# Two-layer decoder trunk: the gated y of both query halves split in the next head's first pass, and TensorE in place of transfers for turning the attention weights of the last two and a half heads

## The chip, the cores and the metric

The kernel runs on one core of one Trainium2 chip. The metric is the device time of one execution in microseconds (us), as the median of several runs. A core has a matrix engine (TensorE, PE in the profile, with its weight loads as PEld), VectorE (DVE), ScalarE (ACT), GpSimd (POOL), a queue engine that issues transfers (SyncE, SP), and 16 DMA engines that carry them. Each engine works through its own queue in order and waits on semaphores for the others.

## What is computed

Two pre-norm residual layers on x (1024 rows of 1024 float32), then a final RMSNorm. The change lies wholly in the second layer, gated attention with a forgetting bias:

```python
def fox_mixer(h, w_in, b_f, w_out):              # 16 heads of width 64
    u = h @ w_in                                 # q, k, v, gate, f_logit
    cum = jnp.cumsum(jax.nn.log_sigmoid(f_logit + b_f), axis=1)
    logits = einsum("bqhd,bkhd->bhqk", q, k) * scale
    logits = logits + (cum[q] - cum[k])          # causal mask after it
    p = jax.nn.softmax(logits, axis=-1)
    o = einsum("bhqk,bkhd->bqhd", p, v)
    y = o * jax.nn.silu(gate)
    return y @ w_out
```

The first layer is a gated linear recurrence (RG-LRU) with three large projections. It takes the time up to about 440 us and isn't touched.

## The kernel before

**Arithmetic.** Products of float32 are made of fp32r parts: a value is split into a high part, a cast (`to_hi`, line 87 on ACT), and a low part, a subtraction of the cast from the value (`to_lo`, line 98). A product is three matmuls: high by high, high by low, low by high (`gps`, `ups`, `vps`, `ops`). The attention weights are split into `ph` and `pl` and multiplied by V in one precision, so they need two.

**Heads, halves and passes.** Attention goes over 16 heads (`hd`); two heads make a pair and share 128 partitions. Each head has two query halves, `c` = 0 and 1, of 512 rows in four blocks of 128. For one half, `maxima` (line 750) makes the logits `S` from `T` (keys) and `U` (queries) on TensorE, adds the mask and takes row maxima on DVE (line 773), and takes the exponential on ACT (line 778), which also gives the row sums. Row tiles are `p` for the two shorter rows of a half and `pp` for the two longer ones. `weigh` (line 815) then turns the weights so that keys lie on partitions, splits them (lines 87 and 98) and multiplies them by V into `O`. The loop over heads runs two passes per head: in the first, `weigh(hd, 0)` stands beside `maxima(hd, 1)`; in the second, `weigh(hd, 1)` beside `maxima(hd+1, 0)`.

**How weights are turned.** Two ways exist. TensorE transposes 128x128 blocks into `pt` (helper on line 61). Or `turn_row` (line 726): DVE transposes 32x32 blocks (`STREAM_TRANSPOSE`, line 733), SP writes the tile to device memory (`turnd`, line 738 for c = 1 and 740 for c = 0), and four reads bring it back into `pp` with the blocks in place (line 745). `by_dma` (line 721) says which halves use the second way for their two longer rows; before, it was all but head 0's first half. The two shorter rows always go by TensorE.

**Gate and y.** At the end of a head the row sums are inverted, transposed (line 791), copied to `rc`, written to memory (`recd`, line 794) and read back as a broadcast over partitions (`recb`, line 803). POOL then multiplies the gate `sg` by it (`scale`, line 813), and, after the odd head of a pair, `yo` by the gate (`gated`, line 911). `yo` is the half's output: ACT copies one head's part of `O` into it (line 901), DVE adds the other. There are two buffers of the tag `yo`, one for each half; the next pair's even head writes into them again.

**Putting y away.** For the pairs of heads up to 11, `put_away` (line 917) splits y: ACT casts `yh` from `yo`, DVE subtracts in place in `yo`, and SP writes both parts to `y1d` (line 928). In head 12 `load_y` (line 984) brings them back as `yhh` and `yhl`. The pairs of heads 13 and 15 are split in place (`split_y`, line 979). `partial` (line 998) multiplies y of the first six pairs by the output weights (`wo1`, loads `wf<-in_wo`), adds the residual (`xp`, read on line 1006, added on 1009, stored on 1010). `turned` (line 1029) transposes the result, adds the last two pairs and takes the squares for the norm.

**What sets the order.** The generators `weigh` and `maxima` are stepped by strings (`ORDER` for heads up to 11, `LAST` from 12 on): "0" and "1" step one of the two, and "." steps the projections that fill TensorE in between, and then a `side` generator.

```python
ORDER = "1.0.1.10.1..0", "10.1.0.10.1.0.0"
LAST = "1..0.1..10..1..0", "10..1.0..10..1.0..0"
```

Before, the side generator of a second pass is `settle` (line 930): it fetches the sums at its third ".", scales and gates the first half at its fourth, and puts that half away at its fifth. The side generator of a first pass is `put_later` (line 941): at its fourth "." it puts away the second half of the head before. Both matter only behind odd heads up to 11. All transfers of this layer go out of SP's one queue, in the order of the program, over eight DMA semaphores in rotation. Tiles of the tags `wf` (three buffers), `S` and `R` (two) are shared by many steps.

Of the kernel before, what the change touches and what calls it, by code (L numbers as in the profile page):

```python
# [17 lines left out]
P = 128  # L18
SEQ = 1024
HALF = 512  # L20
# [13 lines left out]
def f32(ap):  # L34
    return ap.bitcast(F32)
# [3 lines left out]
def trunk(ctx: ExitStack, tc: tile.TileContext, xt, w0, wg, wo0, pc, gn, gf, w1, wv, wf, bf, wo1, out):  # L39
# [44 lines left out]
    def to_hi(hi, src, eng, scale=None):  # L84
        if eng is nc.scalar:
            if scale is None:
                nc.scalar.copy(hi, src)  # L87
            else:
                nc.scalar.activation(hi, src, AF.Copy, scale=scale)
        elif eng is nc.gpsimd:  # L90
            nc.gpsimd.tensor_scalar(hi, src, 1.0 if scale is None else scale, 0.0, ALU.mult, ALU.add)
        elif scale is None:
            eng.tensor_copy(hi, src)
        else:
            eng.tensor_scalar(hi, src, scale, None, ALU.mult)

    def to_lo(lo, src, hi, eng):
        return eng.tensor_tensor(lo, src, f32(hi), ALU.subtract)  # L98
# [80 lines left out]
    with ExitStack() as l0:  # L179
# [33 lines left out]
        first = ([], [])  # L213
# [288 lines left out]
    with ExitStack() as l1:  # L502
# [170 lines left out]
        first = values(0, [])  # L673
# [45 lines left out]
            return two_rows[c][:, r * size : r * size + n]  # L719

        def by_dma(hd, c):
            return hd > 0 or c == 1

        written, turns = [None], {}

# [73 lines left out]
        def fetch_sums(hd, b0=0, b1=8):  # L799
            pair, s = hd // 2, hd % 2  # L800
            if s == 0:
                recs[pair] = at.tile([P, SEQ], F32, tag="recb", name="recb", bufs=1)
            nc.sync.dma_start(
                recs[pair][s * HD : (s + 1) * HD, b0 * P : b1 * P],
                recd[hd : hd + 1, b0:b1].rearrange("o b q -> o (b q)").to_broadcast([HD, (b1 - b0) * P]),
            )

        def scale(hd, cs=slice(0, SEQ)):
            rows = slice((hd % 2) * HD, (hd % 2 + 1) * HD)
            for b in range(cs.start, cs.stop, HALF):  # L810
                part = slice(b, b + HALF)
                sg = sgs[hd // 2][rows, part]
                nc.gpsimd.tensor_tensor(sg, sg, recs[hd // 2][rows, part], ALU.mult)  # L813

        def weigh(hd, c, sub=slice(0, HALF)):
# [6 lines left out]
            O = ps.tile([P, HALF], F32, tag="O", name="O")[:, : sub.stop - sub.start]  # L822
            b = 4 * c

            def cover(r):
                first = [max(j, r) for j in range(r + 2)]
                return [(j, (q - b) * P, (r + 2 - q) * P) for j, q in enumerate(first)]

            def packed(pieces):
                units = []  # L830
                for piece in pieces:
                    if not units or sum(w for _, _, w in units[-1]) + piece[2] > HALF:
                        units.append([])
                    units[-1].append(piece)
                return units

            mine = cover(b) if sub.start == 0 else []
            away = cover(b + 2) if sub.stop == HALF else []
            n = len(away) - 1 if by_dma(hd, c) else 0
            mine, away = packed(mine + away[n:]), packed(away[:n])  # L840
            steps = [(z[i : i + 2], z is away) for z in (mine, away) for i in range(0, len(z), 2)]
            count = [0, 2 * sum(map(len, mine + away))]

# [21 lines left out]
            for units, far in steps:  # L865
# [4 lines left out]
                for u, unit in enumerate(units):  # L870
                    n = sum(w for _, _, w in unit)
# [28 lines left out]
            r0, r1 = s * HD, (1 - s) * HD  # L900
# [4 lines left out]
        def gated(hd, c, sub=slice(0, HALF)):  # L905

            if hd % 2 == 0:
                return
            pair = hd // 2
            yo = yos[pair, c][:, sub]  # L910
            nc.gpsimd.tensor_tensor(
                yo, yo, sgs[pair][:, c * HALF + sub.start : c * HALF + sub.stop], ALU.mult
            )
            if hd == 15:
                split_y(c, pair, yo, sub)

        def put_away(hd, c):
            if hd % 2 == 0 or hd > 12:
                return
            pair = hd // 2  # L920
            yo = yos[pair, c]
            yh = at.tile([P, HALF], F32R, tag="xp", name="yh", bufs=2)
            with tc.issue_after(seen[0].ins):
                to_hi(yh, yo, nc.scalar)
            with tc.issue_after(masked[0].ins):
                to_lo(yo.bitcast(F32R), yo, yh, nc.vector)
            for part, y in enumerate((f32(yh), yo)):
                nc.sync.dma_start(y1d[c, pair, part], y)

        def settle(hd):  # L930
            yield
            yield
            with tc.issue_after(written[0].ins):
                fetch_sums(hd)
            yield
            scale(hd)
            gated(hd, 0)
            yield
            put_away(hd, 0)

        def put_later(hd):
            yield
            yield
            yield
            put_away(hd, 1)

        def beside(*gens):
            for _ in itertools.zip_longest(*gens):
# [167 lines left out]
        for hd in range(HEADS):  # L1116
# [20 lines left out]
            first, second = LAST if hd > 11 else ORDER  # L1137
            side = put_later(hd - 1) if hd else iter(())
            run(first, weigh(hd, 0), maxima(hd, 1), fill=fill, side=side)
            drain(side)  # L1140
            if hd == HEADS - 1:
# [106 lines left out]
```

## Time and profile before

| | before |
|---|---|
| runs (us) | 1132.59, 1134.2, 1134.7 |
| median (us) | 1134.2 |
| profiled execution's own time (us) | 1137.31 |
| span in the profile (us) | 1135.5 |
| mean granted TensorE clock | 0.981 |
| busy, share of the span | PE 97%, PEld 82%, DVE 70%, ACT 51%, POOL 15% |
| device memory read / written | 87.02 / 39.65 MB |

The profile is of one execution. Times in its rows are us from the start of the span. "Busy" counts an engine's instructions from start to end; the time of an instruction that waits is idle time of its engine, and the releaser named beside it is what ended the wait. A matmul row names its output and its two operands, with the size of the weights and of the moving tile. The chain of waits is the work that ended last, followed back from the end. The granted clock is TensorE's, as a share of full speed.

### The profile page before, as it was taken

The numbers are of one execution on the slowest core, as the hardware profiler recorded it, in microseconds if no ns is written. First come the engines' busy times: TensorE is split into PE (matmuls) and PEld (weight loads), VectorE is DVE, ScalarE is ACT, GpSimd is POOL, SyncE is SP. The second block draws the span as 40 slices with busy tenths as digits, with TensorE's granted clock in tenths as the row PEclk, the third lists the DMA queues.
The fourth block names the chain that finished last, engine by engine and source line by source line (L and its number), as shares of the span: only waits on it lengthen the run. The fifth ranks groups of instructions, "written<-read, shape, count | busy, mean of one in ns | idle before, by whom it ended". The sixth has DMA issues, their size and how long they took to land.

```text
span 1135.5 us, 15920 instructions
## 1 busy us (share of the span) xinstructions
PE 1097.4 (97%) x5627; PEld 928.5 (82%) x5627; DVE 797.6 (70%) x1291; ACT 581.6 (51%) x1038; POOL 171.8 (15%) x120
## 2 busy tenths in 40 slices
PE   9999999999999999999999999899998999988998
PEld 7787888888888888978788988788887898867776
DVE  8898765677566897667787487874777847647545
ACT  8587344445445656445555355554555534424335
POOL 2312212212111102311111011101111010110010
PEclk9999999999999999999999999999998999989899
DMA  5111111111112124355767267672676735897554
GB/s 217 59 61 41 53 42 52 47 51 53 41 52 66 45 81 145 93 162 151 217 175 201 78 179 200 194 194 84 176 199 181 197 94 169 311 259 225 177 177 185
DMA packets 107511, 152.89 MB, mean 135 GB/s; under 512 B 27844, under 2 KB 59204, under 8 KB 107432
## 3 DMA queue, kind: packets, MB, share of 16 engines
q1 hardware_dynamic: 107432, 151.88, 45.1%
q8 instruction: 44, 0.72, 0.3%
q14 instruction: 35, 0.29, 0.1%
HBM read 87.02 MB, written 39.65 MB: 112 GB/s over the span
## 4 chain that ended last, share of the span: by engine, by line
PE 78%; DMA 7%; DVE 5%; issue 4%; ACT 3%; POOL 1%; SPq 1%; ACTq 0%; DVEq 0%; POOLq 0%
PE gps L57 28%; PE ops L57 16%; PE ups L57 10%; PE vps L57 8%; PE S L57 5%; PE O L57 5%; PE turn L57 3%; PE gate L57 2%; PE pt L61 2%; DMA wf<-in_w 1%; DVE pl L98 1%; DMA recd<-rc 1%; DMA recb<-recd 1%; DMA yhl<-y1d 1%; ACT pp L778 1%
## 5 line engine op out<-in xcount | busy, mean ns | idle before, releaser
L57 PE MATMUL gps<-hh,wh 128*128 128x512 f32 x576 | 231.0, 401 | 0.0
L57 PE MATMUL gps<-hh,wl 128*128 128x512 f32 x576 | 227.0, 394 | 0.1
L57 PE MATMUL gps<-hl,wh 128*128 128x512 f32 x576 | 226.4, 393 | 0.0
L87 ACT CAST wh<-wf 128x512 fp32r<-128x512 f32 (+2 forms) x156 | 94.1, 607 | 131.7 <-PE ops L57 42.7
L98 POOL TENSOR_TENSOR wl<-wf,wh 128x512 fp32r<-128x512 f32 (+1 forms) x60 | 99.3, 1659 | 378.7 <-ACT wh L87 261.9
L57 PEld LDWEIGHTS gps<-hl,wh 128*128 128x128 f32 x576 | 109.1, 189 | 23.8
L57 PEld LDWEIGHTS gps<-hh,wl 128*128 128x128 f32 x576 | 109.6, 190 | 18.7 <-POOL wl L98 0.6
L57 PEld LDWEIGHTS gps<-hh,wh 128*128 128x128 f32 x576 | 109.6, 190 | 18.5
L813 POOL TENSOR_TENSOR sg<-sg,recb 64x512 f32<-64x512 f32 x32 | 44.7, 1414 | 494.7 <-DMA recb<-recd 494.7
L773 DVE CUSTOM_DVE_ANT_0 S<-S,mask 128x512 f32<-128x512 f32 (+7 forms) x128 | 97.3, 760 | 27.3 <-PE S L57 26.4
L57 PE MATMUL S<-T,U 128*128 128x512 f32 (+7 forms) x384 | 94.9, 357 | 10.7 <-ACT pp L778 10.7
L778 ACT ACTIVATE pp<-S,m 128x512 f32<-128x512 f32 (+1 forms) x64 | 54.3, 849 | 90.3 <-DVE m L773 90.3
L57 PEld LDWEIGHTS S<-T,U 128*128 128x128 f32 (+1 forms) x384 | 69.4, 195 | 26.5 <-ACT pp L778 13.5
L57 PE MATMUL O<-ph,v 128*128 128x256 f32 x320 | 82.3, 286 | 2.6 <-ACT ph L87 2.6
L98 DVE TENSOR_TENSOR wl<-wf,wh 128x512 fp32r<-128x512 f32 x96 | 66.3, 697 | 25.6 <-ACT wh L87 25.4
L98 DVE TENSOR_TENSOR pl<-pp,ph 128x512 fp32r<-128x512 f32 x94 | 64.5, 718 | 27.7 <-ACT ph L87 24.4
L375 DVE TENSOR_TENSOR x<-x,ops 128x512 f32<-128x512 f32 x80 | 54.2, 682 | 41.4 <-PE ops L57 41.4
L57 PE MATMUL O<-pl,v 128*128 128x256 f32 x320 | 81.0, 290 | 0.4 <-DVE pl L98 0.3
L57 PE MATMUL vps<-wh,hh 128*128 128x256 f32 (+1 forms) x256 | 74.6, 292 | 3.2 <-DVE sg L699 1.4
L57 PE MATMUL ups<-hh,wl 128*128 128x512 f32 x192 | 75.1, 391 | 0.8 <-POOL wl L98 0.8
L57 PE MATMUL ups<-hh,wh 128*128 128x512 f32 x192 | 75.7, 395 | 0.1
L57 PE MATMUL ups<-hl,wh 128*128 128x512 f32 x192 | 75.2, 392 | 0.2 <-DVE hl L232 0.2
(170 smaller groups left out, 2398.7 us busy)
## 6 DMA issues: line engine op xcount, KB each, us to landing
wf<-in_w SPq DMA_DIRECT2D x100, 256.0 KB
turnd<-turn SPq DMA_DIRECT2D x32, 448.0 KB
pp<-turnd SPq DMA_DIRECT2D x64, 224.0 KB
wf<-in_wo SPq DMA_DIRECT2D x64, 128.0 KB
U<-qkh SPq DMA_DIRECT2D x64, 128.0 KB
T<-qkh SPq DMA_DIRECT2D x28, 256.0 KB
turnd<-turn SPq DMA_DIRECT2D x15, 384.0 KB
pp<-turnd SPq DMA_DIRECT2D x60, 96.0 KB
```

The costliest lines, as they stand in the source:

```text
L57: pe[0] = nc.tensor.matmul(*args, **kw)
L61: pe[0] = nc.tensor.transpose(*args)
L87: nc.scalar.copy(hi, src)
L98: return eng.tensor_tensor(lo, src, f32(hi), ALU.subtract)
L375: nc.vector.tensor_tensor(x, x, pt, ALU.add)
L773: masked[0] = nc.vector.tensor_tensor_reduce(S[:, :n], S[:, :n], mask[:, SEQ - n :], -1.0, -NEG, ALU.add, ALU.min, accum_out=m)
L778: seen[0] = nc.scalar.activation(p, S[:, :n], AF.Exp, bias=m, scale=-1.0, accum_out=sums[:, i : i + 1])
L813: nc.gpsimd.tensor_tensor(sg, sg, recs[hd // 2][rows, part], ALU.mult)
```

## The change

Two edits. In the first, `put_away` of the first half leaves `settle`, and `put_later` does both halves: the first at its third "." and the second at its fifth, in the first pass of the head that follows. In the second, `by_dma` holds from head 0's second half to head 13's first half only; the second half of head 13 and both halves of heads 14 and 15 are turned by TensorE. `cover` now takes a range of row blocks, so that halves that TensorE turns get pieces of up to four row blocks, 512 wide, in one matmul into `O`; this holds for the first half of head 0 too.

```diff
         def by_dma(hd, c):
-            return hd > 0 or c == 1
+            return 0 < 2 * hd + c < 27
...
-            def cover(r):
-                first = [max(j, r) for j in range(r + 2)]
-                return [(j, (q - b) * P, (r + 2 - q) * P) for j, q in enumerate(first)]
+            def cover(r0, r1):
+                first = [max(j, r0) for j in range(r1)]
+                return [(j, (q - b) * P, (r1 - q) * P) for j, q in enumerate(first)]
...
-            mine = cover(b) if sub.start == 0 else []
-            away = cover(b + 2) if sub.stop == HALF else []
-            n = len(away) - 1 if by_dma(hd, c) else 0
-            mine, away = packed(mine + away[n:]), packed(away[:n])
+            if by_dma(hd, c):
+                away = cover(b + 2, b + 4)
+                mine = packed(cover(b, b + 2) + away[-1:])
+                away = packed(away[:-1])
+            else:
+                mine, away = packed(cover(b + sub.start // P, b + sub.stop // P)), []
...
             scale(hd)
             gated(hd, 0)
-            yield
-            put_away(hd, 0)

         def put_later(hd):
-            yield
-            yield
-            yield
-            put_away(hd, 1)
+            for c in range(2):
+                yield
+                yield
+                put_away(hd, c)
```

Over the whole program TensorE's transposes of weights rise from 262 to 316, DVE's 32x32 transposes fall from 62 to 52, and SP's transfers fall from 760 to 732: the reads `pp<-turnd` from 124 to 104 and the writes of `turnd` from 47 to 39. The matmuls into `O` were 512 of 256 columns and 128 of 128; now they are 450 of 256, 118 of 128, 10 of 384 and 26 of 512. In the changed kernel the lines behind `cover` stand two further down (the copy into `yo` is line 903).

The order on ACT, from the end of head 1's second pass into head 2's first. `ph` and `pp` are weights of attention, `pt` those that TensorE turned, `yh` the cast of y, `yo` the half's output, `wh` weights of a projection, `S` the logits, `t` and `sg` the gate. Before:

```order
L87 CAST ph<-pp 128x256
L87 CAST yh<-yo 128x512
L87 CAST wh<-wf 128x512
L901 COPY yo<-O 64x512
L701 ACTIVATE t_4857<-sg_4653 128x512
L778 ACTIVATE pp,sums<-S,m 128x1024
L87 CAST ph<-pt 128x512
L778 ACTIVATE pp,sums<-S,m 128x896
L778 ACTIVATE p,sums<-S,m 128x768
L87 CAST ph<-pp 128x8x2x32
L87 CAST ph<-pp 128x256
L87 CAST yh<-yo 128x512
```

and after:

```order
L87 CAST ph<-pp 128x256
L87 CAST wh<-wf 128x512
L903 COPY yo<-O 64x512
L701 ACTIVATE t_4848<-sg_4649 128x512
L778 ACTIVATE pp,sums<-S,m 128x1024
L87 CAST ph<-pt 128x512
L778 ACTIVATE pp,sums<-S,m 128x896
L87 CAST yh<-yo 128x512
L778 ACTIVATE p,sums<-S,m 128x768
L87 CAST ph<-pp 128x8x2x32
L87 CAST ph<-pp 128x256
L87 CAST qkh<-gps_4889 128x512
```

The first cast of y has moved from the end of the second pass to behind the second exponential of the next first pass, and the one for the second half to behind the rows shown, just ahead of the next copy into `yo`.

The order on ACT in head 13's second half; `yhh` is the cast of y of head 13's pair. Before:

```order
L87 CAST wh<-wf 128x512
L778 ACTIVATE p,sums<-S,m 128x128
L87 CAST ph<-pp 128x8x2x32 x2
L87 CAST wh<-wf 128x256
L87 CAST ph<-pp 128x8x2x32
L87 CAST ph<-pp 128x256
L87 CAST yhh<-yo 128x512
L901 COPY yo<-O 64x512
```

and after:

```order
L87 CAST ph<-pt 128x512
L87 CAST ph<-pt 128x384
L87 CAST wh<-wf 128x512
L778 ACTIVATE p,sums<-S,m 128x128
L87 CAST yhh<-yo 128x512
L87 CAST wh<-wf 128x256
L87 CAST ph<-pt 128x384
L903 COPY yo<-O 64x512
```

The casts of transferred weights (`ph<-pp`) are gone, casts of weights that TensorE turned stand in their place, and the cast of y has moved ahead of the last of them.

The order on SP at the same place; `recd` and `recb` are the inverse sums on their way out and back, `x1d` the residual, `turnd` the turned weights in memory. Before:

```order
L635 DMA U_3596<-cumd 2x512
L108 DMA wf<-in_wo 128x512
L794 DMA recd<-rc 8x128
L1010 DMA x1d<-xp 128x512 x2
L745 DMA pp<-turnd_4012 32x8x224 x4
L740 DMA turnd_4011<-turn 128x768
L108 DMA wf<-in_wo 128x256
L803 DMA recb<-recd 64x1024
L1006 DMA xp<-x1d 128x512
```

and after:

```order
L635 DMA U_3596<-cumd 2x512
L794 DMA recd<-rc 8x128
L1010 DMA x1d<-xp 128x512 x2
L803 DMA recb<-recd 64x1024
L1006 DMA xp<-x1d 128x512
```

Between the write of the sums and their read stand two writes of the residual and nothing more; the four reads, the write of turned weights and a load of output weights no longer stand between them.

## Prediction

> **What bounds the kernel now.** I read the page first, then TensorE's instructions in order of time with the idle time ahead of each, then the granted clock in stretches cut around those idle times, and last the chain of waits and the rows of ScalarE (ACT), VectorE (DVE), GpSimd (POOL) and the DMA queue (SP) around them.
>
> The page's busy row (us, share of the span, instructions):
>
> ```profile
> PE 1097.4 (97%) x5627; PEld 928.5 (82%) x5627; DVE 797.6 (70%) x1291; ACT 581.6 (51%) x1038; POOL 171.8 (15%) x120
> ```
>
> TensorE bounds the program, so a microsecond counts only where TensorE stands still, runs at a lower clock, or gets more work. Its rows after the long idle times (start, duration, instruction, and in brackets the idle time and what ended it):
>
> ```profile
> 568.54 0.50 PE L57 MATMUL S<-T,U 128*128 128x512 f32 x1 [3.36 <-ACT pp L778]
> ...
> 627.19 0.51 PE L57 MATMUL vps<-wh,hh 128*128 128x256 f32 x1 [0.68 <-DVE sg L699]
> ...
> 712.51 0.70 PE L57 MATMUL S<-T,U 128*128 128x512 f32 x1 [3.70 <-ACT pp L778]
> ...
> 856.54 0.80 PE L57 MATMUL S<-T,U 128*128 128x512 f32 x1 [3.19 <-ACT pp L778]
> ...
> 915.73 0.39 PE L57 MATMUL vps<-wh,hh 128*128 128x256 f32 x1 [0.69 <-DVE sg L699]
> ...
> 1008.90 0.39 PE L57 MATMUL O<-ph,v 128*128 128x256 f32 x1 [2.55 <-ACT ph L87]
> 1009.63 0.58 PE L57 MATMUL O<-pl,v 128*128 128x256 f32 x1 [0.34 <-DVE pl L98]
> ...
> 1013.80 0.80 PE L57 MATMUL ops<-yhh,wh 128*128 128x512 f32 x1 [1.89 <-DVE xp L1009]
> ...
> 1051.68 0.80 PE L57 MATMUL ops<-yhh,wh 128*128 128x512 f32 x1 [5.36 <-ACT wh L87]
> ...
> 1098.49 0.47 PE L57 MATMUL turn<-ident,x 128*128 128x128 f32 x1 [2.45 <-DVE xp L1009]
> ```
>
> Those at 568.54, 712.51 and 856.54 lie in the second passes of heads 1, 5 and 9 and wait for ACT. The stretches (length, then busy us and instructions of PE, PEld, DVE, ACT, POOL, then the granted clock, DMA share, GB/s) show what follows an idle time:
>
> ```profile
> 569.30:572.70 3.40, 3.40 (x10) 2.73 (x10) 2.11 (x4) 1.10 (x2) 0.49 (x1) 0.50 0.34 137
> 623.90:627.30 3.40, 1.77 (x11) 1.31 (x11) 3.24 (x5) 0.82 (x3) 0.55 (x1) 1.00 0.84 228
> 627.30:630.70 3.40, 3.40 (x17) 3.40 (x17) 2.60 (x5) 2.22 (x5) 0.51 (x1) 0.50 0.77 260
> 712.60:716.00 3.40, 3.40 (x9) 2.85 (x10) 2.84 (x4) 0.82 (x2) 1.14 (x1) 0.51 0.44 174
> 856.00:862.80 6.80, 6.26 (x19) 5.30 (x19) 4.03 (x6) 2.06 (x5) 1.78 (x1) 0.50 0.24 90
> 912.30:915.70 3.40, 2.54 (x14) 1.67 (x12) 3.38 (x6) 1.68 (x4) 0.08 (x1) 1.00 0.80 237
> 1009.60:1019.80 10.20, 8.28 (x25) 6.83 (x26) 5.08 (x7) 1.95 (x4) 4.06 (x3) 0.50 0.86 236
> 1098.30:1101.70 3.40, 3.21 (x10) 2.67 (x11) 0.94 (x3) 0.51 (x2) 0.00 (x0) 0.51 0.42 154
> ```
>
> After an idle time TensorE runs at half clock for 3.4 us or a multiple of it: a 3.4 us stretch that was 52% busy (1.77 of 3.40) was followed by one at 0.50, one that was 75% busy (2.54) kept 1.00. So each stall costs its idle time and half of TensorE's busy time in the stretch behind it.
>
> Why ACT is late in head 1, from the chain of waits and from ACT's own row:
>
> ```profile
> 551.81 4.66 DMA recd<-rc
> ...
> 556.48 3.50 DMA recb<-recd
> ```
>
> ```profile
> 564.04 0.62 ACT L87 CAST yh<-yo 128x512 fp32r<-128x512 f32 x1 [4.97 <-POOL yo L911]
> ```
>
> The reciprocal sums go out to memory and back, POOL scales the gate and multiplies y, and the cast of y stands in ACT's queue ahead of the softmax work that TensorE needs: ACT is held 4.97 us and TensorE 3.36.
>
> **The change part by part.** The sum is made against the profiled execution (span 1135.5, its own time 1137.3) and then taken off the median of the runs, 1134.2, which is 3.1 lower.
>
> *A, the cast of y leaves the second passes of heads 1, 5 and 9.* Idle 3.36 + 3.70 + 3.19 = 10.25 goes. Behind ACT the next in line is the scaled gate on POOL, which no longer has anyone waiting in that pass. What is late next is DVE, which now has to work while POOL runs; the first and the last row here are pairs of the same subtraction without and with POOL at work:
>
> ```profile
> 613.63 1.29 DVE L98 TENSOR_TENSOR wl<-wf,wh 128x512 fp32r<-128x512 f32 x2
> ...
> 620.23 2.54 POOL L813 TENSOR_TENSOR sg<-sg,recb 64x512 f32<-64x512 f32 x2 [27.62 <-DMA recb<-recd]
> ...
> 622.31 2.69 DVE L98 TENSOR_TENSOR wl<-wf,wh 128x512 fp32r<-128x512 f32 x2 [3.08 <-ACT wh L87]
> ```
>
> One such subtraction stands ahead of the masked maximum there and takes (2.69 - 1.29) / 2 = 0.7 longer, so I leave 0.7 of idle time at each (bounds 0 to 1.4): 2.1. The half-clock stretches behind hold 3.40 + 3.40 + 6.26 = 13.1 of busy time, of which half, 6.5, was lost; a remainder of 0.7 keeps the stretch at about 80% busy, above the 75% that kept the clock. A = -(10.25 - 2.1) - 6.5 = **-14.6** (bounds -16.8 and -8).
>
> *B, heads 3, 7 and 11.* There TensorE did not wait for the cast, but DVE's subtraction of y stood just ahead of sg (L699), which ended the idle 0.68 and 0.69: 1.4 goes. The stretch 623.9 to 627.3 would rise to 1.77 + 0.68 = 2.45 of 3.40, 72%, nearer the 75% that kept the clock than the 52% that did not: half of 3.40, 1.7, goes too. B = **-3.1** (0 to -3.1).
>
> *C, both splits now lie in the first pass of heads 2 to 12.* ACT, DVE and two DMAs of y for the first half come into a pass that has those for the second half already, and each is moved past SP's writes of turned rows. One more subtraction for DVE, 1.29 / 2 = 0.65 by the row above, six times, is 3.9; nothing if idle time hides it. The first pass of head 4, in a stretch of 25 us:
>
> ```profile
> 650.00:675.00 25.00, 24.94 (x140) 21.28 (x139) 20.56 (x41) 15.05 (x33) 2.78 (x2) 1.00 0.66 186
> ```
>
> DVE is busy for 20.56 of 25 and ACT for 15.05, so most of it is hidden: **+1.0** (0 to 3.9).
>
> *D, 54 more transposes on TensorE:* 14 in each of three second halves (heads 13, 14, 15), 6 in each of two first halves. A group of eight that is on the path now, from the chain, and all of them on the page:
>
> ```profile
> 1038.06 0.88 PE pt L61 x8
> ...
> L61 PE MATMUL pt<-ident,p 128*128 128x128 f32 x224 | 32.7, 274 | 0.3
> ```
>
> 0.88 / 8 = 0.11 each in a row, 5.9 in all; with nothing overlapped 54 x 0.274 = 14.8. They stand in groups of 3 to 8, so I take **+5.9** (to 14.8). [...] The matmuls into O become half as many of twice the width, the same columns: nothing. The 20 reads, 8 writes and 10 VectorE transposes that go were on no path but those below.
>
> *E, head 13's second half.* The idle times at 1008.90 and 1009.63 wait for casts of transfers, the one at 1013.80 for DVE behind them. From the chain, SP's rows and ACT's:
>
> ```profile
> 1003.34 4.82 DMA pp<-turnd
> ...
> 1019.29 1.01 PE O L57 x6
> ```
>
> ```profile
> 998.91 0.27 SPq L794 DMA_DIRECT2D recd<-rc  x1
> ...
> 1001.34 2.61 SPq L745 DMA_DIRECT2D pp<-turnd  x4
> ...
> 1005.13 0.73 SPq L803 DMA_DIRECT2D recb<-recd  x1
> ```
>
> ```profile
> 1015.67 0.62 ACT L87 CAST yhh<-yo 128x512 fp32r<-128x512 f32 x1 [4.34 <-POOL yo L911]
> ```
>
> Idle 2.55 + 0.34 + 1.89 = 4.8 goes, and half of the 8.28 busy at half clock, 4.1. Of the new waits, ACT's cast of y (yhh) now stands ahead of the last cast of the weights, and it waits for recb by way of POOL. TensorE comes to the last products, now at 1019.29, 8.9 earlier and 14 transposes (1.5) later: 1011.9. On SP the four reads between recd and recb are gone, so recb can go out some 4 earlier and yhh run at 1011 to 1012, just in time. E = **-8.9** (bounds -3.0, rival 1, and -8.9).
>
> *F, the stall at 1051.68.* It waits for weights whose buffer came free late:
>
> ```profile
> 1046.24 4.75 DMA wf<-in_wo
> ```
>
> The buffer's release does not move much. The load shares its time with a write and four reads that go; at recb's 3.50 it would be 1.2 quicker, and TensorE arrives about 1 later by D. So the idle time shrinks by 2 and its half clock stays. F = **-2.0** (bounds +1.5 and -8).
>
> *G, the stall at 1098.49.* DVE waits for a cast of y that waits for recb; recd went out late, after an add's buffer was written back beside four reads of turned rows that go:
>
> ```profile
> 1079.05 2.54 SPq L745 DMA_DIRECT2D pp<-turnd  x4
> ...
> 1089.35 0.28 SPq L794 DMA_DIRECT2D recd<-rc  x1
> ```
>
> At most 2.45 and half of 3.21, 4.1, can go; recd can move up by about the 2.5 that those reads took to issue, about the idle time. I take **-2.5** (+1.5 to -4.1).
>
> Sum: -14.6 - 3.1 + 1.0 + 5.9 - 8.9 - 2.0 - 2.5 = **-24.2**. 1134.2 - 24.2 = **1110.0** (1113.1 in a profiled execution).
>
> **The rivals.** *1, the wait moves to yhh in head 13.* If recb lands as late as now, yhh still ends at 1016.3, two casts and a subtraction follow, and TensorE, there at 1011.9, starts the last products at 1017.8: it stands for 5.9, E falls to -3.0, and stretches at half clock behind it take about 2.5 more: **1118**. For it: recb needs recd's landing first, and the stretch is full of reloads of y. Against it: the reads ahead of recb are gone.
>
> *2, the first passes take the time back.* If the added cast and subtraction (0.62 + 0.68) are on the path in all six, C is 7.6: **1117**. Against it: the idle time of both, above.
>
> *3, transposes do not keep the clock up.* A stretch with eight has 0.88 of 3.40 that would not count, which leaves 74%; if that fell under the limit, about ten groups would each cost half of 3.40: +17, **1127**. [...] The trace so far speaks against a cost: the group of eight at 1038.06 was followed by no stretch at half clock.
>
> *4, slower: the first half's y is put away too late for its buffer.* The copy of the next head's O into that buffer, ACT's row, now waits for the write of y, whose subtraction follows DVE's second transpose (rows of DVE and ACT in head 4; the third, from the chain, is a reload of y, the same size as the write):
>
> ```profile
> 657.08 1.11 DVE L733 STREAM_TRANSPOSE turn<-pp 128x896 f32<-128x896 f32 x1
> ...
> 662.31 0.58 ACT L901 COPY yo<-O 64x512 f32<-64x512 f32 x1 [0.31 <-PE O L57]
> ...
> 981.63 5.83 DMA yhl<-y1d
> ```
>
> The write can start near 658.2 + 0.65, so 3.5 are left for it to land. At recb's 3.50 there is no wait. At 5.83, which the reload of y takes, ACT waits 2.3 in each of six passes with a half-clock stretch of 1.7 behind: 24, all of the gain. At 6.5 it is 6 x (3.0 + 1.7) = 28: **1138**. It decides from 5.9 us on. The DMA share of 0.66 in that pass speaks against so long a landing.
>
> **How the numbers follow.** Forecast 0.64; rival 1 0.18, rival 2 0.08, rival 3 0.05, rival 4 0.04, and 0.01 for a smaller loss. The range is 1102 (A, F and G at better ends) to 1124 (rivals 1 and 2 and the sum with D near its upper end); rivals 3 and 4 lie outside. About 0.2% is what a measurement of this kernel can tell from no change: faster 0.92, same 0.03, slower 0.05.
>
> **What would show it.** In the changed profile the cast of y waits for POOL no more, the idle 3.36, 3.70 and 3.19 are under 1 and have no half clock behind them; 20 fewer reads of turned rows stand on SP; the transposes still take 0.11 in a row. I am wrong if ACT's copy into yo waits for a DMA, if a stall of several us stands behind yhh near 1012, or if the granted clock falls where transposes are thick.

## The result, and the profile after

The changed kernel takes 1114.93 us (median of four runs, 1114.79 to 1115.17) where the kernel before took 1133.98 (1132.59 to 1134.7, four runs): a ratio of 0.9834, 95% interval 0.9817 to 0.9851. The profiled execution took 1114.79 with a span of 1113.0, which is 22.5 less than the span before; the mean granted clock rose from 0.981 to 0.995. One execution of experiment 1 (1787.65 us, granted clock 0.556) and one of experiment 6 (2166.41 us at 0.986) lie far above the others and are left out, and since the only trace of experiment 1 is of that execution, no row of it is used.

The busy row of the page after:

```profile
PE 1088.5 (98%) x5645; PEld 921.1 (83%) x5645; DVE 792.1 (71%) x1280; ACT 579.9 (52%) x1037; POOL 171.8 (15%) x120
```

TensorE's rows in order of time, at the places shown of before and at the new ones (in brackets the idle time and what ended it):

```profile
565.90 0.92 PE L57 MATMUL S<-T,U 128*128 128x512 f32 x3 [0.55 <-ACT pp L778]
578.46 0.45 PE L57 MATMUL S<-T,U 128*128 128x384 f32 x1 [0.39 <-ACT pp L778]
590.81 0.39 PE L57 MATMUL O<-pl,v 128*128 128x256 f32 x1 [0.68 <-DVE pl L98]
...
706.26 0.50 PE L57 MATMUL S<-T,U 128*128 128x512 f32 x1 [1.07 <-ACT pp L778]
...
845.87 0.92 PE L57 MATMUL S<-T,U 128*128 128x512 f32 x3
...
1028.72 0.79 PE L57 MATMUL ops<-yhh,wh 128*128 128x512 f32 x1 [3.15 <-ACT wh L87]
...
1075.92 0.55 PE L57 MATMUL turn<-ident,x 128*128 128x128 f32 x3 [0.95 <-DVE xp L1009]
```

The stalls of 3.36, 3.70 and 3.19 are down to 0.55, 1.07 and none. Those of head 13's second half (2.55, 0.34 and 1.89) have gone. That at 1051.68 is now the one at 1028.72, 3.15 in place of 5.36, and 2.45 became 0.95. New are 0.39 at 578.46 and 0.68 at 590.81, and others like them in the second passes of heads 4 to 10. In stretches (columns as in the prediction):

```profile
565.90:569.30 3.40, 3.40 (x18) 2.97 (x19) 2.91 (x5) 1.06 (x2) 0.00 (x0) 1.00 0.36 138
...
706.30:709.70 3.40, 3.40 (x19) 2.97 (x19) 2.92 (x5) 1.06 (x2) 0.00 (x0) 1.00 0.43 169
1004.30:1011.10 6.80, 6.80 (x35) 5.80 (x34) 4.32 (x8) 2.57 (x5) 0.00 (x0) 1.00 0.44 153
1027.80:1034.60 6.80, 5.41 (x16) 4.36 (x17) 2.63 (x5) 1.85 (x6) 0.98 (x1) 0.50 0.53 188
```

The clock is full where it was half; after 480 us only the stall at 1028.72 still has half clock behind it (and the program's end). Where the time went is read by comparing the starts of the same matmul, the first into `S` of a half, in both traces:

| place | before, from and to | after, from and to | longer by |
|---|---|---|---|
| first pass, head 2 | 560.86, 579.25 | 561.03, 575.06 | -4.36 |
| head 6 | 704.50, 723.19 | 700.87, 715.41 | -4.15 |
| head 10 | 849.04, 868.54 | 841.60, 855.03 | -6.07 |
| second pass, head 3 | 607.27, 648.93 | 604.24, 644.12 | -1.78 |
| head 7 | 751.07, 793.23 | 743.96, 784.52 | -1.60 |
| head 11 | 896.39, 936.53 | 883.55, 923.06 | -0.63 |
| second pass, head 2 | 579.25, 594.07 | 575.06, 591.04 | +1.16 |
| head 4 | 662.11, 676.79 | 657.31, 673.16 | +1.17 |
| head 6 | 723.19, 737.87 | 715.41, 730.76 | +0.67 |
| head 8 | 806.43, 821.31 | 797.72, 813.89 | +1.29 |
| head 10 | 868.54, 883.22 | 855.03, 870.38 | +0.67 |
| second pass, head 13 | 990.84, 1020.14 | 977.37, 998.43 | -8.24 |
| from there to the end | 1020.14, 1135.5 | 998.43, 1113.0 | -0.79 |

These add up to -22.7. The rest of the program is 0.2 longer in all.

### The profile page after: what moved, and what is told of

Same layout as the page of the kernel before. It is cut to its first block, busy times and chain, and to the rows that moved or that the text cites. A ratio compares the mean times of both kernels' runs of the same rounds, so it can differ in the third digit from the quotient of the medians.

```text
span 1113.0 us, 15892 instructions
## 1 busy us (share of the span) xinstructions
PE 1088.5 (98%) x5645; PEld 921.1 (83%) x5645; DVE 792.1 (71%) x1280; ACT 579.9 (52%) x1037; POOL 171.8 (15%) x120
## 4 chain that ended last, share of the span: by engine, by line
PE 76%; DVE 7%; DMA 6%; issue 5%; ACT 4%; SPq 1%; POOL 1%; ACTq 0%; DVEq 0%; POOLq 0%
PE gps L57 26%; PE ops L57 16%; PE ups L57 10%; PE vps L57 7%; PE S L57 5%; PE O L57 4%; PE gate L57 3%; PE turn L57 2%; PE pt L61 2%; DVE pl L98 2%; ACT pp L778 1%; DMA T<-qkl 1%; DVE S L773 1%; DMA U<-qkh 1%; DMA turnd<-turn 1%
## 5 line engine op out<-in xcount | busy, mean ns | idle before, releaser
L57 PE MATMUL S<-T,U 128*128 128x512 f32 (+7 forms) x384 | 92.6, 350 | 4.0 <-ACT pp L778 4.0
L98 DVE TENSOR_TENSOR wl<-wf,wh 128x512 fp32r<-128x512 f32 x96 | 68.6, 720 | 22.6 <-ACT wh L87 22.5
L57 PE MATMUL O<-pl,v 128*128 128x256 f32 (+3 forms) x302 | 77.2, 290 | 2.2 <-DMA T<-qkl 1.2
L57 PE MATMUL O<-ph,v 128*128 128x256 f32 (+3 forms) x302 | 78.8, 289 | 0.0
L57 PE MATMUL ops<-yh,wh 128*128 128x512 f32 x192 | 75.2, 392 | 0.0
```

Of the source, the lines that this page charges most:

```text
L57: pe[0] = nc.tensor.matmul(*args, **kw)
```

## The experiments

Theory, taken from the prediction: ACT stood behind the cast of y, which waited for GpSimd, and so TensorE stood at the head of the next first pass; head 13 waited for its own transferred weights; the two gains add up. Rivals: lateness handed on from one place to the other, VectorE's or SP's part of putting y away, dear transposes. New is the question of what made the second passes of heads 2 to 10 longer. Each group of four kernels shared a chip and the runs of the kernel before on it (medians 1137.33, 1136.9 and 1137.79). That kernel's runs reach from 1131.9 to 1143.0 there, so the ratio to it is given.

**1. Only the move of y.** The kernel before with the move of y alone; `by_dma` and `cover` stay.

```diff
             gated(hd, 0)
-            yield
-            put_away(hd, 0)
...
         def put_later(hd):
-            yield
-            yield
-            yield
-            put_away(hd, 1)
+            for c in range(2):
+                yield
+                yield
+                put_away(hd, c)
```

> Only the move of the splitting of y into the next first pass; the weights of the last heads go by transfers as before. By stretches of the two profiles the move accounts for -14.6 (stalls at the head of the first passes of heads 2, 6 and 10), -4.0 (second passes of heads 3, 7 and 11) and +4.9 (second passes of heads 2, 4, 6, 8 and 10), -13.7 in all. If the terms add up, this kernel is 9.2 slower than the changed one: 1124, and its profile shows the stalls at the head of the first passes under 1.2 us and those of head 13's second half and after (4.8, 5.4 and 2.5 us idle) still there. Rival: the stalls late in the program came of lateness handed on from the earlier heads; then they are gone here too, and the time is near 1115.

Measured: ratio 0.9895 (0.9862 to 0.9928), 1125.1. That is 0.0061 to 0.0069 above the changed kernel's ratios (first measurement and experiment 5), 7 to 8 us where 9.2 were expected and none by the rival. So the gains late in the program are not lateness handed on; whether the stalls at the head of the first passes went here can't be read, since there is no trace of an execution like the others.

**2. Only TensorE's turning.** The changed kernel with the same lines put back.

```diff
             gated(hd, 0)
+            yield
+            put_away(hd, 0)
...
         def put_later(hd):
-            for c in range(2):
-                yield
-                yield
-                put_away(hd, c)
+            yield
+            yield
+            yield
+            put_away(hd, 1)
```

> Only the weights of the last two and a half heads turned by TensorE; y is put away as before. If the terms add up, -9.2 from the second half of head 13 on (-8.9 there, -1.9 and -3.1 at the two later stalls, +4.7 for the transposes): 13.7 slower than the changed kernel, 1128 to 1129, with the stalls of 3.4, 3.7 and 3.2 us at the head of the first passes of heads 2, 6 and 10 as before. Rival: the second passes of heads 2 to 10 are longer here too, since something other than the moved splits made them so; then 1130 and more.

Measured: 1129.29, ratio 0.9927 (0.9904 to 0.9949). The stalls at the head of the first passes are back, and nothing of them was handed on:

```profile
568.93 1.46 PE L57 MATMUL S<-T,U 128*128 128x512 f32 x3 [3.69 <-ACT pp L778]
...
711.94 1.49 PE L57 MATMUL S<-T,U 128*128 128x512 f32 x4 [3.49 <-ACT pp L778]
...
857.41 0.91 PE L57 MATMUL S<-T,U 128*128 128x512 f32 x3 [2.93 <-ACT pp L778]
```

The two parts take off 1.05% and 0.73%, together 1.78%, where both at once take off 1.66% (first measurement) and 1.74% (experiment 5). They add up within the intervals. The second passes of heads 2 to 10, by the same comparison of starts, are 1.2 longer than before here, where the changed kernel has 5.0: most of that belongs to the move of y.

**3. Both halves at the third step.**

```diff
         def put_later(hd):
-            for c in range(2):
-                yield
-                yield
-                put_away(hd, c)
+            yield
+            yield
+            put_away(hd, 0)
+            put_away(hd, 1)
```

> The changed kernel with both halves of y put away at the third step of the fill instead of the third and the fifth. It asks what made the second passes of heads 2, 4, 6, 8 and 10 longer (0.7 to 1.3 us each). Theory 1, the order on ACT: with the second cast at the fifth step, two casts of turned weights stand ahead of the exponential that TensorE waits for (idle 0.39 in each of the five passes); here only one does, and 2 us go: 1113. Theory 2, GpSimd's scaling of the gate falls on DVE's last splitting of weights (2.75 us for two in place of 1.71): that does not depend on it, and the time stays at 1115. Rival 3: two casts and two subtractions in a row hold up the exponential behind them: 1117 or more.

Measured: 1117.82, ratio 0.9842 (0.9801 to 0.9882): no gain. The waits of 0.39 behind ACT have gone in all five passes, as theory 1 said, but the waits for DVE's `pl` (0.68) stand in heads 2, 4 and 10, as theory 2 said they would, and the first pass of head 2 is 0.9 longer than in the changed kernel. By the starts, the five second passes are 1.1 shorter together and the five first passes ahead of them 2.0 longer, so rival 3 is real in part. The order on ACT makes the small waits and not most of the loss.

**4. The kernel before, once more.**

> The kernel before once more, for a second profile. The first profiled execution took 3.1 us longer than the median of the runs, the changed kernel's profiled one took just its median. If that was the run and not the profiling, this profiled execution takes about 1134, with the idle times of TensorE the same within 1 us and less half clock (the stretch at 856 is 3.4 long in place of 6.8, or another one is gone). If profiling adds it, 1137 again with the same stretches.

Measured: 1136.22 for this profiled execution, 1.1 under the median of that chip's runs, so profiling adds nothing that can be seen. The three stalls are 3.48, 2.92 and 3.05, much as in the first profile (3.36, 3.70, 3.19), but the half clock behind them lies otherwise:

```profile
568.40:575.20 6.80, 6.36 (x19) 5.39 (x20) 4.03 (x6) 1.96 (x5) 1.68 (x1) 0.50 0.23 86
711.80:718.60 6.80, 6.05 (x18) 5.09 (x18) 4.00 (x7) 2.27 (x5) 1.78 (x1) 0.50 0.29 109
858.50:861.90 3.40, 3.40 (x10) 2.81 (x9) 2.23 (x4) 1.10 (x2) 0.60 (x1) 0.51 0.35 140
```

It lasts two stretches of 3.4 us, two and one, where the first profile had one, one and two. The six stalls, of 2.92 to 3.70 us, cost one or two stretches of 3.4 by where they fell: 1.7 or 3.0 to 3.2 us. Where TensorE was busy for all of the first 3.40 at half clock (from 569.30 and 712.60 in the first profile, from 858.50 here) there was one; where the idle time reached into it (2.86 busy from 856.00 in the first profile, 2.96 and 2.65 from 568.40 and 711.80 here) there were two. The stretches of one execution start whole multiples of 3.41 from one another (from 569.3 to 712.6 in the first profile 42 of them, from 568.4 to 858.5 here 85), and counted from the start of the span the grids of the two executions lie 0.9 apart (569.3 and 568.4).

**5. The changed kernel, once more,** for the three kernels on its chip.

> The changed kernel once more, on the chip of the three kernels that follow, for comparison with them. If what spreads the runs of the kernel before over several us is the half clock that its stalls set off, sometimes one stretch of 3.4 us and sometimes two, this kernel, which has few stalls, spreads by less than 1 us again and its median is 1115; if the spread is the chip's, it spreads as the kernel before does.

Measured: 1116.96 (1115.16 to 1118.68), ratio 0.9826 (0.9784 to 0.9869). It spreads by 3.5 us in four runs where the kernel before spreads by 9.0 in thirteen. Less, but not under 1: the half clock is not all of the spread, since runs at 1115.46 and 1118.46 have the same mean clock, 0.997.

**6. The cast alone put back.** ACT's cast of the first half's y goes back to `settle`'s fifth step, while the subtraction and the writes stay in the next first pass.

```diff
...
             gated(hd, 0)
+            yield
+            cast_y(hd, 0)
...
```

> The changed kernel with one instruction put back: ACT's cast of the first half's y stands where it stood before, at the end of the second pass; the subtraction on DVE and the two writes stay in the next first pass. Theory: the cast, which waits for GpSimd on ACT, was what held TensorE at the head of the first passes of heads 2, 6 and 10. Then all of it comes back, some 3.3 us of idle time and the half clock behind it in each of the three, and the time is 1127 to 1130. Rival: the subtraction on DVE or the writes on SP held up the chain; then nothing comes back and the time is 1115 to 1117.

Measured: 1129.8 (1126.1 to 1135.8), ratio 0.9935 (0.9912 to 0.9957). One instruction per pair of heads brings back 12 to 13 us. TensorE's stalls:

```profile
568.38 1.11 PE L57 MATMUL S<-T,U 128*128 128x512 f32 x3 [2.84 <-ACT pp L778]
...
712.57 0.79 PE L57 MATMUL S<-T,U 128*128 128x512 f32 x1 [3.40 <-ACT pp L778]
...
856.31 1.22 PE L57 MATMUL S<-T,U 128*128 128x512 f32 x2 [3.23 <-ACT pp L778]
```

and ACT at the first of them, where the cast waits for GpSimd and the exponential comes 3.2 us behind it:

```profile
563.96 0.62 ACT L87 CAST yh<-yo 128x512 fp32r<-128x512 f32 x1 [4.55 <-POOL yo L913]
...
567.12 1.11 ACT L778 ACTIVATE pp<-S,m 128x1024 f32<-128x1024 f32 x1 [0.76 <-DVE m L773]
```

The subtraction on DVE and the writes on SP stay where the changed kernel has them, so it was the cast.

**7. The halves swapped.** The second half put away at the third step, the first at the fifth.

```diff
         def put_later(hd):
-            for c in range(2):
-                yield
-                yield
-                put_away(hd, c)
+            yield
+            yield
+            put_away(hd, 1)
+            yield
+            yield
+            put_away(hd, 0)
```

> The changed kernel with the two halves swapped: the second half of y put away at the third step of the fill, the first half at the fifth, just ahead of ACT's copy of the next O into the first half's buffer. This makes the wait of the prediction's rival 4 on purpose. In the changed kernel's profile the write of the half that goes at the fifth step goes out at 577.1 and lands 4.8 later, at 581.9, and the copy stands at 575.3: if the copy waits for the landing, ACT stands for 6 to 7 us in each of six passes, TensorE for most of that with two stretches at half clock behind it, 6 x (5 + 3) = 48: about 1160. If the buffer's release costs nothing that matters, 1115.

Measured: 1118.37, ratio 0.9832 (0.9798 to 0.9866): no wait. ACT's copies into `yo` waited for no write here. In head 2 the copy starts at 576.05 and the first half's writes go out only at 577.06 and 577.76, so the next pair's first half does not take the buffer of the first half. That it takes whichever was given back first, here the one that went at the third step, fits this and experiment 9; the rows don't number the buffers.

**8. One scaling of the gate for a pair of heads.** GpSimd's `scale` does nothing behind even heads up to 12 and takes both heads' rows behind the odd one. What is computed stays the same.

```diff
         def scale(hd, cs=slice(0, SEQ)):
+            if hd < 14 and hd % 2 == 0:
+                return
-            rows = slice((hd % 2) * HD, (hd % 2 + 1) * HD)
+            rows = slice((hd % 2) * HD if hd > 13 else 0, (hd % 2 + 1) * HD)
```

> The changed kernel with GpSimd's scaling of the gate left out behind even heads up to 12 and done for both heads of a pair at once behind the odd one (128 partitions in place of 64, as many instructions there). Theory 2 for the longer second passes of heads 2 to 10: the scaling runs beside DVE's last splitting of weights, which takes 2.75 us in place of 1.3 to 1.7, and TensorE waits 0.56 to 0.68 in three of the five; without it these go, some 2 to 3 us: 1112 to 1113, and the waits of 0.39 behind ACT stay. Rival: DVE is late by its own work; then 1115.

Measured: 1112.40 (1111.41 to 1113.66), ratio 0.9782 (0.9748 to 0.9816); 4.6 under the changed kernel on the same chip, 2.6 by the spans (1113.4 and 1110.8). The intervals of the two ratios overlap, so the reading rests on the rows. In the changed kernel GpSimd's scaling and DVE's splittings at the end of head 2's second pass stood so:

```profile
587.50 2.97 POOL L813 TENSOR_TENSOR sg<-sg,recb 64x512 f32<-64x512 f32 x2 [22.64 <-DMA recb<-recd]
```

```profile
585.98 0.69 DVE L98 TENSOR_TENSOR pl<-pp,ph 128x512 fp32r<-128x512 f32 x1
588.01 2.75 DVE L98 TENSOR_TENSOR pl<-pp,ph 128x512 fp32r<-128x512 f32 x2 [1.34 <-ACT ph L87]
```

and here, where GpSimd does nothing:

```profile
586.24 0.69 DVE L98 TENSOR_TENSOR pl<-pp,ph 128x512 fp32r<-128x512 f32 x1
588.27 1.03 DVE L98 TENSOR_TENSOR pl<-pp,ph 128x512 fp32r<-128x512 f32 x2 [1.34 <-ACT ph L87]
```

The last two splittings take 1.03 alone and 2.75 beside the scaling, TensorE's wait of 0.68 for them is gone, and the five second passes are 3.6 shorter than in the changed kernel by their starts (0.96, 0.83, 0.33, 1.15, 0.33). In the kernel before the scaling ran beside DVE too, but earlier against the pass:

```profile
589.63 2.98 POOL L813 TENSOR_TENSOR sg<-sg,recb 64x512 f32<-64x512 f32 x2 [19.84 <-DMA recb<-recd]
```

```profile
589.76 1.70 DVE L98 TENSOR_TENSOR pl<-pp,ph 128x512 fp32r<-128x512 f32 x1
591.79 1.71 DVE L98 TENSOR_TENSOR pl<-pp,ph 128x512 fp32r<-128x512 f32 x2 [0.33 <-ACT ph L87]
```

Counted from the start of that pass (579.25 before, 575.06 after, from the table) the scaling began at 10.4 before and at 12.4 after. Before, it held back one splitting that had time, and part of the last two; after, it fell on the last two whole. SP's rows show what delayed it:

```profile
582.61 0.28 SPq L794 DMA_DIRECT2D recd<-rc  x1
...
585.78 0.49 SPq L803 DMA_DIRECT2D recb<-recd  x1
```

before, and after:

```profile
579.27 0.28 SPq L794 DMA_DIRECT2D recd<-rc  x1
...
582.80 0.48 SPq L803 DMA_DIRECT2D recb<-recd  x1
```

The sums went out 0.85 later in the pass (3.36 and 4.21 from its start) and were asked for 1.2 later (6.53 and 7.74); the remaining 0.85 is the transfer. The first 0.85 comes from the order on DVE, which copies the sums to `rc`. TensorE starts to transpose them 2.74 from the start of the pass in both kernels. Before, that copy stood ahead of two splittings of weights that TensorE turned:

```profile
582.30 0.28 DVE L793 COPY rc<-tr 8x128 f32<-8x128 f32 x1
...
583.14 1.28 DVE L98 TENSOR_TENSOR pl<-pt,ph 128x512 fp32r<-128x512 f32 x2
```

After, it stands behind them, as on ACT the exponential now stands behind the two casts of the same weights:

```profile
577.76 1.29 DVE L98 TENSOR_TENSOR pl<-pt,ph 128x512 fp32r<-128x512 f32 x2 [0.48 <-ACT ph L87]
578.97 0.27 DVE L793 COPY rc<-tr 8x128 f32<-8x128 f32 x1
```

It is so in all five passes (3.05 and 3.91 from the start). The order is not all: in heads 4 and 8 of experiment 6 the copy is back at 3.05, and the scaling still starts at 11.92 and 12.76, where it was 10.11 and 10.64 before. Which transfer holds it up there isn't shown. Why a splitting takes longer beside the scaling isn't shown either; two together are late by 1.7 (2.75 and 1.03), a little more than one of GpSimd's two products takes (2.97 / 2 = 1.5).

**9. Both halves late:** the first at the fifth step, the second at the sixth, so that no buffer of `yo` is given back early.

```diff
         def put_later(hd):
-            for c in range(2):
-                yield
-                yield
-                put_away(hd, c)
+            yield
+            yield
+            yield
+            yield
+            put_away(hd, 0)
+            yield
+            put_away(hd, 1)
```

> The changed kernel with the first half of y put away at the fifth step of the fill and the second at the sixth. The experiment with the halves swapped did not make the wait that rival 4 of the prediction speaks of, because the next copy into yo takes whichever of the two buffers is given back first. With both late there is no early one: the write that goes at the fifth step goes out at 577.1 and lands at 581.9 in the changed kernel's profile, and the copy is due at 575.3. If the copy waits for the landing, ACT stands 6 to 7 us in each of six passes, TensorE for 4 to 6 of it, with one or two stretches at half clock behind: 6 x 7.5 = 45, about 1160 (1140 at the least). If it does not wait, 1117.

Measured: 1128.95, ratio 0.9919 (0.9888 to 0.995). What ACT's copies into `yo` waited for in all (us, times), in the changed kernel and here:

```profile
  DMA y1d<-yo: 0.7, 2
```

```profile
  DMA y1d<-yo: 17.7, 5
  DMA T<-qkl: 2.3, 1
```

The wait of rival 4 is real: up to 3.76 in a pass (head 2), and it costs 12 us against experiment 5 (11 by the ratios), a quarter of what was expected; the second passes of heads 2 to 10 are 10.5 longer together than in the changed kernel. Here the copy stands behind two casts and an exponential on ACT, so that TensorE loses 1.7 at the first one and not 5 or 6:

```profile
582.84 0.58 ACT L903 COPY yo<-O 64x512 f32<-64x512 f32 x1 [3.76 <-DMA y1d<-yo]
```

```profile
584.70 0.51 PE L57 MATMUL S<-T,U 128*128 128x256 f32 x2 [0.77 <-ACT pp L778]
...
586.45 0.38 PE L57 MATMUL O<-pl,v 128*128 128x256 f32 x1 [0.89 <-DVE pl L98]
```

**10. TensorE from the second half of head 6 on,** in `by_dma`.

```diff
-            return 0 < 2 * hd + c < 27
+            return 0 < 2 * hd + c < 13
```

> The changed kernel with TensorE turning the weights from the second half of head 6 on: 140 transposes more (456 in place of 316), and as much fewer transfers and transposes on DVE. It measures the term for a transpose on TensorE. From the second half of head 13 on, the profiles show about 4.7 us more work for 54 transposes, matmuls into O included: 0.087 each, so 140 would add 12: 1129 (a little less if DVE's relief takes stalls away). At 0.11 each they add 15: 1132. [...] Rival: transposes do not hold the granted clock up; then stretches at 0.5 appear among heads 7 to 12, where the changed kernel has none, and the mean clock falls under 0.98.

Measured: 1128.43, ratio 0.9914 (0.9885 to 0.9943), span 1126.8. Against experiment 5 that is 10.0 by the ratios, 11.5 by the medians and 13.4 by the spans for 140 transposes: 0.07 to 0.10 each with everything that goes along. The clock stays full throughout the added ones:

```profile
715.00:915.00 200.00, 194.03 (x1109) 166.67 (x1108) 125.29 (x253) 100.67 (x220) 23.06 (x17) 1.00 0.37 100
915.00:1000.00 85.00, 85.00 (x497) 74.85 (x496) 46.52 (x95) 36.09 (x80) 3.83 (x3) 1.00 0.51 158
```

Whether transposes alone would keep the clock up is not settled by this, since a group of eight (0.88) is about a quarter of a stretch of 3.4 and may be too little to show.

**11. One scaling, and y put away at the first and the fourth step,** on top of experiment 8.

```diff
         def put_later(hd):
-            for c in range(2):
-                yield
-                yield
-                put_away(hd, c)
+            put_away(hd, 0)
+            yield
+            yield
+            yield
+            put_away(hd, 1)
```

> The kernel with one scaling of the gate for a pair of heads, and with the halves of y put away at the first and the fourth step of the fill, so that one cast of turned weights and not two stands ahead of the exponential on ACT. The five waits of 0.39 in the second passes of heads 2 to 10 should go: 2 us off that kernel's 1112.4, 1110. Rival: ACT's earlier cast of y waits for GpSimd or holds up the exponential in the first pass instead: 1112 or more.

Measured: 1114.63 (1114.56 to 1117.94), ratio 0.9798 (0.9767 to 0.9829): not better than experiment 8. The waits of 0.39 went in heads 2, 6 and 10 and stayed in heads 4 and 8. In exchange the subtraction of y now stands ahead of the masked maximum on DVE at the start of the first pass, and TensorE waits there:

```profile
570.09 0.94 PE L57 MATMUL S<-T,U 128*128 128x512 f32 x4 [0.95 <-DVE pl L98]
...
848.64 0.71 PE L57 MATMUL S<-T,U 128*128 128x512 f32 x2 [0.95 <-DVE pl L98]
```

**12. Head 13's second half by transfers again,** heads 14 and 15 by TensorE.

```diff
-            return 0 < 2 * hd + c < 27
+            return 0 < 2 * hd + c < 28
```

> The changed kernel with head 13's second half turned by transfers again, and heads 14 and 15 still by TensorE: one part of the second edit undone. Theory: the stalls of 2.6, 0.3 and 1.9 us and the half clock there wait for this half's own reads of turned rows and come back, 8.9, less the 14 transposes saved, 1.2: 7.7 slower than the changed kernel, 1123 to 1125. Rival: they came of the traffic of heads 14 and 15 or of lateness handed on; then it is 1114 to 1117.

Measured: 1122.93 (1121.39 to 1125.77), ratio 0.9859 (0.9824 to 0.9895): 6.0 slower than experiment 5 by the medians (3.8 by the ratios, which allow for the two chips and whose intervals overlap), and head 13's second pass is 5.8 longer than in the changed kernel (26.9 and 21.1). Two of the three stalls are back just as they were, the third only in part:

```profile
1000.39 0.39 PE L57 MATMUL O<-ph,v 128*128 128x256 f32 x1 [2.56 <-ACT ph L87]
1001.12 0.58 PE L57 MATMUL O<-pl,v 128*128 128x256 f32 x1 [0.34 <-DVE pl L98]
...
1003.82 0.80 PE L57 MATMUL ops<-yhh,wh 128*128 128x512 f32 x1 [0.41 <-DVE xp L1009]
```

So the first two belong to this half's own transfers. Of the third, 1.89 before, 1.5 had another cause, which the transfers of heads 14 and 15 or the moved loads may be; that wasn't separated.

## Why the prediction came out as it did

The time fell inside the range, 4.9 above the forecast. By the terms of the sum:

- **A (-14.6): right, in cause and in size.** -4.36 - 4.15 - 6.07 = -14.6. Experiment 6 shows the cause, ACT's cast that waits for GpSimd. The place was named loosely: TensorE stands at the head of the first passes of heads 2, 6 and 10, behind the cast at the end of the second passes before them. What I left for the next delay, 0.7 each, came out as 0.55, 1.07 and 0. The size is that of one pair of executions: by experiment 4 the half clock behind these three stalls was 7.9 in place of 6.5 another time.
- **B (-3.1): right in cause, too small,** -4.0, beyond its own bound. The waits for `sg` have gone and so has the half clock. But head 3 gained 1.78 where 0.68 + 1.7 were forecast, since a wait of 0.31 for `v` (L575) is new there, and head 7, for which the term had nothing, gained 1.60: the profile before has a stretch at half clock there, from 770.70 to 774.10, 3.26 busy. In experiment 4's profile head 7 has such a stretch and head 3 has none, so this term too goes with the execution.
- **C (+1.0, up to 3.9): the step that was wrong.** The first passes of heads 2 to 12 hide the added cast and subtraction as I argued from their idle time. (The stretch from 650 to 675, taken for the first pass of head 4, holds nearly all of its second pass too, which starts at 662.11; the 20.56 and 15.05 are averages over both. Rival 2's 7.6 should be 6 x 1.30 = 7.8.) But the loss, +5.0, is in the second passes behind them, which the step didn't look at. I had counted the work of ACT and DVE, and not what the move does to the order on them and to the next step in line: the inverse sums go out and come back later, and GpSimd's scaling, until then harmless, falls on DVE's last splitting (experiment 8, 3.6 of the 5.0). The rows for it were there: term A used the pair 1.29 and 2.69 for a subtraction without and with GpSimd at work, and looked for it in one place only. The waits of 0.39 on ACT are a second, smaller part (experiment 3).
- **D (+5.9): slightly too much.** Outside the stalls, the program from head 13's second half on is 4.6 to 4.9 longer (-9.0 in the table, where the stalls alone give -13.9; 0.3 lies behind the last matmul), about 0.09 for each of 54; experiment 10 gives 0.07 to 0.10 over 140. The wider matmuls into `O` are in this, and were put at nothing.
- **E (-8.9): right.** That pass lost all of its 4.8 idle and 4.1 of half clock; with its 14 transposes it is 8.24 shorter. Rival 1 did not come: `recb` was asked for 9.3 from the start of the pass in place of 14.3, ACT's cast of yhh waited 0.68 in place of 4.34, and no wait is left on TensorE there. Experiment 12 brought back the two stalls at the weights and 5.8 us of the pass.
- **F (-2.0): right. G (-2.5): right in size, not in cause.** At F idle time went from 5.36 to 3.62 (3.15 and 0.47) and half clock from 2.85 to 2.7 (half of the 5.41 busy above), -1.9; at G from 4.1 in all to 0.95, -3.1. But `recd` did not move up by the time of the reads: it went out 37.67 after the matmul that ends stall F before (1051.68 to 1089.35) and 37.52 after it now (1028.72 to 1066.24), and the matmul that waits at G came 46.81 and 47.20 after. TensorE waits less there because it has more to do on the way (45.78 busy in place of 44.36, 16 transposes more), which is D counted from the other side.
- **Rival 4 was real, and just missed.** The copy waited for the write twice, 0.7 in all; with the first half put away two steps later and the second half one step later (experiment 9) the wait costs 11 to 12 us. The mechanism had one error, that the next pair's first half takes the first half's own buffer (experiment 7), and its price was too high.

Against the profiles the sum was -24.2 and the measured change -22.5: C was 4.0 too small, and B, D and G gave about 2.5 of that back. That the sum came so near is in part luck. The other 3.2 of the 4.9 come from taking a sum made on one execution off the median of others: the profiled execution of before lay 3.1 above its runs, the profiled one after at the median of its own. By the medians the change is -19.1 and not -22.5. Part of this is likely the lot that the half clock draws. Over the 31 runs of the kernel before on the three chips of the experiments, the 7 with a mean clock of 0.981 or less have a median of 1140.2 and the 11 with 0.985 or more one of 1134.4; the profiled execution before had 0.981. For the runs beside it no clock is on record.

## What to carry to other kernels

An instruction that waits in the queue of an engine which others wait for can cost them most of its wait, whatever its own length (before, 4.97 on ACT and 3.36 on TensorE for a cast of 0.62); look for a later place in the same queue where its input is already there. When such a step is moved, follow the order of the rows around it and its transfers too, since what they push back by a microsecond can land on another engine's critical row a pass later. And on a kernel with stalls near the length of a stretch at half clock (3.4 us), take a difference of profiles only to within the half clock that moves from run to run (6.5 and 7.9 us behind the same three stalls in the two profiles of before), or profile before twice.

## What was not expected of the hardware

- Stalls of about the same length at the same place (3.36 and 3.48) had one stretch at half clock behind them in one execution and two in the other, 1.7 and 3.2 us, by where they fell on a grid of 3.41 us that lay elsewhere in each (experiment 4).
- Two subtractions on DVE take 1.03 alone and 2.75 beside GpSimd's product, so a GpSimd that is 15% busy decides 2.6 us of the run by the spans (experiment 8).
- With a wait of 3.76 us ahead of one copy on ACT, TensorE lost only 1.7 (experiment 9): what counted was what stood behind the waiting instruction.
